# The gate-up combination of the sampled rows, issued one feature pair later

## The chip, the core and the metric

The kernel runs on one core of one Trainium2 chip. The metric is the device time of one execution in microseconds; the times given for a kernel are of several executions, and the median is the one to compare.

## The reference, cut to what matters

A two-layer decoder trunk is applied to 512 prompt rows and to 32 sampled rows (8 sequences of 4), both of width 1024. Each layer has a mixing part (four token mixers, an input and an output projection) and a feed-forward part. The change touches the feed-forward part of the sampled rows alone:

```python
gate, up = jnp.split(rms_norm(x, p['g_ffn_pre']) @ p['w_gu'], 2, axis=-1)
x = x + rms_norm((jax.nn.silu(gate) * up) @ p['w_down'], p['g_ffn_post'])
```

`w_gu` is 1024 x 5632 (2816 gate columns, then 2816 up columns), `w_down` is 2816 x 1024. In the kernel a feature is a block of 128 of the 2816 columns, so there are 22, handled two at a time as a feature pair.

## The kernel before

**The prompt rows** set the shape of the feed-forward stage. `prompt` walks over the features in three chunks (0 to 7, 8 to 15, 16 to 21). For each pair f, f+1 it loads 1 MB of gate weights and 1 MB of up weights into the two buffers of `raw` (SyncE issues the loads, line 202), splits each into a high and a low part (`whi` by ScalarE on line 194, `wlo` by VectorE on line 197), and multiplies: `dense_fm` makes 24 products of 512 columns per feature and side, 96 for a pair. All matmuls are issued by the helper on line 128; in the rows these products write `acc`. ScalarE and VectorE then form silu(gate) times up (`th`, lines 1368 to 1370) and split it (`h`, lines 1372 and 1373). After each chunk the down projection follows (`project`, or `project_last` for the third chunk), with its own weights through `raw` (line 214).

**The sampled rows** go beside this. For features 0 to 9 a background generator (`sample_ffn`) loads its own weights (`rws`). From feature F0 = 10 on, the sampled rows use the weights which the prompt rows have in `raw` already: `raw_cols` calls `gate_up(f, 0)` on the gate weights and `gate_up(f, 1)` on the up weights before it splits them. Each call makes 8 small float32 products with `quads`, every one into 32 rows of a PSUM tile with tag `sx` (three banks); the trace shows each float32 product as two records, so a call has 16. ScalarE copies the 128 x 256 sum into a half of `obm` (line 1208), a tile of tag `g_s`, which has two buffers.

**The combination** of a pair is `swiglu`. Four float32 products (8 records) with 32 columns of constants add up the four row groups and turn the result, with `obm` as the weights that are loaded; they write `o2`, a PSUM tile of tag `ps` (two banks). ScalarE takes the tanh (`sth`, line 1178), and two VectorE instructions form silu(gate) times up (lines 1179 and 1180) into the 64 columns of `hsa` or `hsb` that `hs2(f)` names. The down projection of the sampled rows reads these columns: `down(c0)` and `also(half)` run `quads` on each raw tile of `w_down`, with `hsa` or `hsb`, and the raw tile can be loaded again only after them and the split.

**The order on an engine** is not the order of the text. The context on line 1484 is opened with `schedule_with_timeline_sim=True`: the instructions of the whole program are put in order before it runs. What the order came to is read from the trace. Once fixed, each engine keeps to it.

In layer 0 the pairs 10, 12 and 14 close the second chunk and the pairs 16, 18 and 20 make up the third; layer 1 is the same. This gives 6 combinations a layer that the change touches, 12 in all.

Of the kernel before, what the change touches and what calls it, by code (L numbers as in the profile page):

```python
# [50 lines left out]
F0 = 10  # L51
# [71 lines left out]
def trunk(ctx, tc, A, O):  # L123
# [3 lines left out]
    def mm(out, lhsT, rhs, start=True, stop=True):  # L127
        T.matmul(out, lhsT, rhs, start=start, stop=stop)  # L128
# [13 lines left out]
    def ps():  # L142
        return psx("ps")

    def psx(tag):
        pool, bufs = banks[tag]
        return pool.tile([128, 512], F32, tag=tag, bufs=bufs, name=tag)
# [17 lines left out]
    def x_at(stage):  # L165
        if stage == 0:
            return x_in
        if stage == 2 * DEPTH:
            return y_out
        return lambda r0, n: xm[stage - 1][r0:r0 + n, :]  # L170
# [73 lines left out]
    def finish_sample(fp, parts, m_s, x_t, stage, gpo, gpr, dst, tag):  # L244


        ss = fp.tile([128, 4], F32, name="sums_s")[:NT]
        junk = fp.tile([128, DM], BF16, name="junk_s")
        for half in range(2):
            o = ps()  # L250
            mm(o[:NT, :], selkg, parts[half])
            hs = slice(512 * half, 512 * half + 512)
            S.activation(junk[:NT, hs], o[:NT, :], AF.Square, accum_out=ss[:, half:half + 1])
            V.tensor_tensor(m_s[:, hs], o[:NT, :], gpo[:NT, hs], op=ALU.mult)
        V.tensor_tensor(ss[:, 2:3], ss[:, 0:1], ss[:, 1:2], op=ALU.add)
        r = rsqrt(fp, ss[:, 2:3], NT, 1, 1.0 / DM, RMS_EPS, tag)
        V.scalar_tensor_tensor(x_t, m_s, r, x_t, op0=ALU.mult, op1=ALU.add)
        SY.dma_start(x_at(stage + 1)(SEQ, NT), x_t)
        if gpr is None:
            return  # L260
        S.activation(junk[:NT], x_t, AF.Square, accum_out=ss[:, 3:4])
        r = rsqrt(fp, ss[:, 3:4], NT, 1, 1.0 / DM, RMS_EPS, tag)
        V.scalar_tensor_tensor(m_s, x_t, r, gpr[:NT], op0=ALU.mult, op1=ALU.mult)
        if dst is None:
            turn(m_s, NT, SEQ)
            return
        for b in range(2):
            o = ps()
            ov = o[:, :4 * NT].rearrange("p (c t) -> p c t", c=4)
            for c in range(4):  # L270
                T.transpose(ov[:, c, :], m_s[:, 128 * (4 * b + c):128 * (4 * b + c) + 128], ident[:NT, :NT])
            S.copy(dst[:, 4 * b:4 * b + 4, :], ov)
# [886 lines left out]
    def sample_ffn(l, cmn, sp, ys, hs_in, share):  # L1159


        def pso():
            return psx("sx")

        def narrow(w, act, groups, c0, n, out):

            for gi, (k0, nk) in enumerate(groups):
                rw = sp.tile([128, 4, 256], F32, tag="rw", bufs=RWB, name="rws")
                SY.dma_start(rw[:, :nk, :n], w[128 * k0:128 * (k0 + nk), c0:c0 + n].rearrange("(k p) f -> p k f", p=128))
                quads(out, act, rw, k0, 0, nk, gi == 0, n, [q for _, q in groups[gi + 1:]])  # L1170
                yield

        def swiglu(ob, dst):
            o2 = ps()
            for i in range(4):
                mm(o2[:, NT * i:NT * i + NT], ob[:, 128 * i:128 * i + 128], selkg)
            t = sp.tile([128, 2 * NT], F32, tag="sth", bufs=2, name="sth")
            S.activation(t, o2[:, 0:2 * NT], AF.Tanh, scale=0.5)  # L1178
            V.scalar_tensor_tensor(t, t, 1.0, o2[:, 0:2 * NT], op0=ALU.add, op1=ALU.mult)  # L1179
            V.scalar_tensor_tensor(dst, t, 0.5, o2[:, 2 * NT:4 * NT], op0=ALU.mult, op1=ALU.mult)  # L1180

        g8 = [(0, 4), (4, 4)]
        gpo = sp.tile([128, DM], F32, tag="g_s", bufs=2, name="g_s")[:NT]
        SY.dma_start(gpo, A["g_mix_post"][l, :].partition_broadcast(NT))
        gpr = sp.tile([128, DM], F32, tag="g_s", bufs=2, name="g_s")[:NT]
        SY.dma_start(gpr, A["g_ffn_pre"][l, :].partition_broadcast(NT))
        m_s = sp.tile([128, DM], F32, tag="m_s", name="m_s")[:NT]
        x_t = sp.tile([NT, DM], F32, name="x_s")
        SY.dma_start(x_t, x_at(2 * l)(SEQ, NT))
        finish_sample(sp, share["parts"], m_s, x_t, 2 * l, gpo, gpr, hs_in, "s")  # L1190
        yield

        m4 = sp.tile([128, DM], F32, tag="m_s", name="m4")
        G.memset(m4, 0.0)
        hsa = sp.tile([128, 16, NT], F32, name="hsa")
        hsb = cmn.tile([128, 8, NT], F32, tag="ys", name="hsb")
        hs = lambda k: hsa[:, k, :] if k < 16 else hsb[:, k - 16, :]
        hs2 = lambda k: (hsa[:, k:k + 2, :] if k < 16 else hsb[:, k - 16:k - 14, :]).rearrange("p f t -> p (f t)")
        obs = {}

        def gate_up(f, i):
            def run(r):
                if i == 0:
                    obs[f] = sp.tile([128, DM], F32, tag="g_s", bufs=2, name="obm")
                o = pso()
                for gi in range(2):
                    quads(o, lambda k: hs_in[:, k, :], r[:, 4 * gi:4 * gi + 4, :], 4 * gi, 0, 4, gi == 0, 256, (4,) if gi == 0 else ())
                S.copy(obs[f][:, 256 * i:256 * i + 256], o[:, :256])
                if i == 1:
                    swiglu(obs.pop(f), hs2(f))  # L1210
            return run

        def down(c0):
            def run(r, k0, nk):
                i0 = max(0, F0 - k0)
                if i0 < nk:
                    o = pso()
                    quads(o, hs, r, k0, i0, nk, True, 512)
                    P = slice(32 * i0, 32 * nk)
                    V.tensor_tensor(m4[P, c0:c0 + 512], m4[P, c0:c0 + 512], o[P, :], op=ALU.add)  # L1220
            return run

        share.update(gate_up=gate_up, down=down, hs=hs)
        wgu = A["w_gu"][l]
        for fp in range(F0 // 2):
            ob = cmn.tile([128, 512], F32, tag="pr", bufs=2, name="ob")
            for i in range(2):
                o = pso()
                yield from narrow(wgu, lambda k: hs_in[:, k, :], g8, DFF * i + 256 * fp, 256, o)
                S.copy(ob[:, 256 * i:256 * i + 256], o[:, :256])  # L1230
            swiglu(ob, hs2(2 * fp))
            yield
        groups = [(k, min(4, F0 - k)) for k in range(0, F0, 4)]
        for cb in range(4):
            o = pso()
            yield from narrow(A["w_down"][l], hs, groups, 256 * cb, 256, o)
            c = slice(256 * cb, 256 * cb + 256)
            P = slice(0, 32 * min(4, F0))
            V.tensor_tensor(m4[P, c], m4[P, c], o[P, :256], op=ALU.add)
            yield  # L1240
        while "last" not in share:
            yield
        share["m4"] = [cmn.tile([128, 512], F32, tag="pr", bufs=2, name="m4h") for _ in range(2)]
        for i in range(2):
            S.copy(share["m4"][i], m4[:, 512 * i:512 * i + 512])
        yield

    def quads(out, act, w, k0, i0, nk, first, n, later=()):


        for i in range(i0, nk):
            mm(out[32 * i:32 * i + 32, :n], act(k0 + i), w[:, i, :n], start=first, stop=all(q <= i for q in later))
# [77 lines left out]
    def prompt(l, fp, share):  # L1330
# [19 lines left out]
        for ci, (f0, nf) in enumerate(chunks):  # L1350
            hb = [yp.tile([128, 2, 2, SEQ], F32R, tag="y", name="h") for _ in range(nf // 2)]
            for fpair in range(nf // 2):
                f = f0 + 2 * fpair
# [10 lines left out]
                for i, c0, n, tag in parts:  # L1364
# [8 lines left out]
                    V.tensor_tensor(hb[fpair][:, 1, i, c0:c0 + n], th[:, :n], hh.bitcast(F32), op=ALU.subtract)  # L1373
                    yield 0.02 * n
            act = lambda k, h, ts_: hb[k // 2][:, h, k % 2, ts_]
            if ci < len(chunks) - 1:
                yield from project(A["w_down"][l], f0, nf, act, m, ci == 0, share)
                continue
# [50 lines left out]
    for l in range(DEPTH):  # L1429
# [5 lines left out]
        with tc.tile_pool(name=f"ffn{l}", bufs=1, reuse_waits="tile") as fp, \  # L1435
# [3 lines left out]
            share = {}  # L1439
# [46 lines left out]
```

## Time and profile before

| | us |
|---|---|
| median of 3 runs | 1473.05 |
| lowest and highest of them | 1468.88 and 1478.08 |
| the profiled execution | 1468.52 |
| its span, first to last instruction | 1466.7 |
| TensorE busy in it | 1399.7 |
| VectorE, ScalarE, GpSimd busy | 819.1, 498.2, 252.2 |

All durations in the text come from the one profiled execution. Its span leaves out what lies before the first and behind the last instruction, 1.8 us. Starts are counted from the begin of the span. TensorE's weight loads (PEld) are listed apart from its matmuls (PE) and overlap them. The end of a matmul is modelled, so that two neighbours overlap in the list: what a matmul costs is read from start to start.

### The profile page before, as it was taken

What the parts mean: (1) busy time and instruction counts of PE and PEld (TensorE: products, weight loads), DVE (VectorE), ACT (ScalarE), POOL (GpSimd) and SP (SyncE); (2) the same over time, 40 slices, a digit from 0 to 9 for tenths busy, and PEclk for the clock granted to TensorE, in tenths of its full rate; (3) what the DMA queues carried; (4) which work ended last, traced back from release to release, by engine and by line L of the source; (5) the groups of instructions that cost most, each with busy time, mean ns of one, the idle gap of its engine ahead of it and who ended that gap; (6) DMA issues with size and microseconds to landing.
All of it is one profiled execution on the core that took longest, in us unless ns stands there. A gap on an engine that the chain in (4) does not pass through costs nothing.

```text
span 1466.7 us, 22999 instructions
## 1 busy us (share of the span) xinstructions
PE 1399.7 (95%) x9274; PEld 1091.6 (74%) x9274; DVE 819.1 (56%) x1624; ACT 498.2 (34%) x978; POOL 252.2 (17%) x271
## 2 busy tenths in 40 slices
PE   6999898999999999999989997989999999999997
PEld 6987687766676777777789876877666677777775
DVE  4996677866424323433769856778664333333344
ACT  4346453322224221222433444543222332222231
POOL 1001155354200000000310011543542000000003
PEclk9999898999999999999999978999999999999999
DMA  6320335787759741323432203367877596213132
GB/s 206 101 88 30 125 129 181 266 292 274 263 179 298 230 137 58 106 67 130 151 123 73 73 29 123 126 218 250 307 277 272 182 300 212 99 58 115 58 133 90
DMA packets 155204, 235.60 MB, mean 161 GB/s; under 512 B 8880, under 2 KB 116410, under 8 KB 155098
## 3 DMA queue, kind: packets, MB, share of 16 engines
q1 hardware_dynamic: 136522, 166.76, 34.6%
q0 software_dynamic: 18432, 67.12, 12.6%
q8 instruction: 73, 1.20, 0.3%
q14 instruction: 33, 0.27, 0.1%
q10 hardware_dynamic: 144, 0.26, 0.0%
HBM read 222.07 MB, written 12.04 MB: 160 GB/s over the span
## 4 chain that ended last, share of the span: by engine, by line
PE 80%; DVE 9%; issue 4%; DMA 2%; ACT 2%; POOL 2%; another core or an unknown queue 1%; SPq 0%; POOLq 0%; DVEq 0%; ACTq 0%
PE acc L128 61%; PE sx L128 10%; PE ps L128 3%; PE s L128 3%; DVE sca L897 2%; DVE wlo L197 1%; PE oT L128 1%; DMA kr<-in_cache_k_dram,ik 1%; POOL rsw L178 1%; DVE m L1326 1%; ACT whi L194 1%; DVE x_t L1319 1%; PE ps L521 1%; PE ps L239 1%
## 5 line engine op out<-in xcount | busy, mean ns | idle before, releaser
L128 PE MATMUL acc<-xhi,whi 128*128 128x512 f32 (+2 forms) x1152 | 410.8, 358 | 3.1 <-issue 1.1
L128 PE MATMUL acc<-xhi,wlo 128*128 128x512 f32 (+2 forms) x1152 | 407.9, 354 | 1.0 <-issue 0.7
L128 PE MATMUL acc<-xlo,whi 128*128 128x512 f32 (+2 forms) x1152 | 407.4, 354 | 1.3 <-DVE xlo L242 1.1
L197 DVE TENSOR_TENSOR wlo<-raw,whi 128x1024 fp32r<-128x1024 f32 x172 | 216.5, 1265 | 187.4 <-ACT whi L194 185.9
L194 ACT CAST whi<-raw 128x1024 fp32r<-128x1024 f32 x178 | 184.8, 1048 | 381.6 <-PE acc L128 324.0
L128 PEld LDWEIGHTS acc<-xhi,whi 128*128 128x128 f32 x1152 | 221.1, 192 | 47.5 <-issue 13.3
L128 PEld LDWEIGHTS acc<-xhi,wlo 128*128 128x128 f32 x1152 | 221.1, 192 | 34.9 <-issue 8.7
L128 PEld LDWEIGHTS acc<-xlo,whi 128*128 128x128 f32 x1152 | 221.3, 192 | 32.8 <-issue 5.3
L128 PE MATMUL acc<-whi,h 128*128 128x512 f32 x704 | 225.4, 397 | 0.3 <-issue 0.3
L128 PEld LDWEIGHTS acc<-whi,h 128*128 128x128 f32 x704 | 132.0, 189 | 45.4 <-issue 11.8
L128 PE MATMUL acc<-wlo,h 128*128 128x512 f32 x352 | 139.2, 397 | 0.0
L1301 POOL TENSOR_TENSOR m<-m,g_g_ffn_post 128x512 f32<-128x512 f32 x14 | 20.0, 1435 | 509.1 <-ACT junk L1300 509.1
L1014 DVE STREAM_TRANSPOSE kt<-kr 128x1024 f32<-128x1024 f32 x64 | 78.3, 1232 | 40.5 <-remote 18.2
L427 DVE SCALAR_TENSOR_TENSOR cacc<-hext,pf,cacc 128x512 f32<-128x512 f32 x120 | 86.9, 746 | 0.8
L1011 POOL DMA_INDIRECT kr<-in_cache_k_dram,ik x64 | 68.6, 1072 | 101.8 <-DVE kt L1014 88.1
L128 PEld LDWEIGHTS acc<-wlo,h 128*128 128x128 f32 x352 | 66.5, 189 | 17.6 <-issue 4.1
L178 POOL TENSOR_TENSOR rsw<-rsw,mhalf 128x1 f32<-128x1 f32 (+2 forms) x62 | 37.3, 604 | 239.4 <-DVE rsw L177 223.4
L1041 POOL DMA_INDIRECT vr<-in_cache_v_dram,iv x64 | 62.1, 970 | 82.0 <-PE sx L128 66.5
L1370 DVE SCALAR_TENSOR_TENSOR th<-th,acc 128x512 f32<-128x512 f32 (+1 forms) x46 | 29.7, 645 | 80.7 <-PE acc L128 80.5
L128 PE MATMUL sx<-kt,qs 128*32 128x128 f32 x1024 | 49.9, 277 | 7.7 <-issue 6.1
L128 PEld LDWEIGHTS sx<-kt,qs 128*32 128x32 f32 x1024 | 30.7, 109 | 24.5 <-issue 18.8
L1179 DVE SCALAR_TENSOR_TENSOR sth<-sth,ps 128x64 f32<-128x64 f32 x22 | 4.8, 219 | 72.7 <-ACT sth L1178 72.7
(426 smaller groups left out, 1855.2 us busy)
## 6 DMA issues: line engine op xcount, KB each, us to landing
raw<-in_w_gu_dram SPq DMA_DIRECT2D x44, 1024.0 KB
raw<-in_w_down_dram SPq DMA_DIRECT2D x20, 1024.0 KB
rws<-in_w_gu_dram SPq DMA_DIRECT2D x40, 512.0 KB
raw<-in_w_in_dram SPq DMA_DIRECT2D x16, 1024.0 KB
raw<-in_w_out_dram SPq DMA_DIRECT2D x8, 1024.0 KB
rwo<-in_w_out_dram SPq DMA_DIRECT2D x16, 512.0 KB
rws<-in_w_down_dram SPq DMA_DIRECT2D x16, 512.0 KB
x<-x_t SPq DMA_DIRECT2D x12, 512.0 KB
```

The source lines that it names most:

```text
L128: T.matmul(out, lhsT, rhs, start=start, stop=stop)
L178: G.tensor_tensor(y, v, mhalf[:P, :n], op=ALU.pow)
L194: S.copy(hi, src)
L197: eng.tensor_tensor(lo, src, hi.bitcast(F32), op=ALU.subtract)
L239: T.transpose(ov[:, c, :], src[:P, 128 * (4 * b + c):128 * (4 * b + c) + 128], ident[:P, :P])
L427: V.scalar_tensor_tensor(a, hext[c][:, t:t + SEQ], pf[:, 8 + 2 * t + c:9 + 2 * t + c], a, op0=ALU.mult, op1=ALU.add)
L897: V.scalar_tensor_tensor(a[:, c], ext[:, c, :, t:t + 4], pf[:, 8 + 2 * t + c:9 + 2 * t + c], a[:, c], op0=ALU.mult, op1=ALU.add)
L1011: G.indirect_dma_start(out=kr, out_offset=None, in_=ck, in_offset=bass.IndirectOffsetOnAxis(ap=ik[:, s, bg:bg + 1], axis=0))
L1014: V.transpose(kt, kr)
L1041: G.indirect_dma_start(out=v.rearrange("p t e -> p (t e)"), out_offset=None, in_=cv, in_offset=bass.IndirectOffsetOnAxis(ap=iv[:, s, a:a + ...
L1301: (V if (t, half) == (3, 1) else G).tensor_tensor(m[t][:, hs], m[t][:, hs], gain[:, hs], op=ALU.mult)
L1370: V.scalar_tensor_tensor(th[:, :n], th[:, :n], 0.5, ou[:, :n], op0=ALU.mult, op1=ALU.mult)
```

## The change

`gate_up` no longer runs `swiglu` when the up half of `obm` is copied. It puts the pair in a list, `late`. The list is emptied by `flush`, which runs `swiglu` on what it finds: at the next call of `gate_up`, behind its products and ahead of its copy, or, for the last pair of a chunk, ahead of the down projection.

```diff
@@ gate_up
                 for gi in range(2):
                     quads(o, lambda k: hs_in[:, k, :], r[:, 4 * gi:4 * gi + 4, :], 4 * gi, 0, 4, gi == 0, 256, (4,) if gi == 0 else ())
+                flush()
                 S.copy(obs[f][:, 256 * i:256 * i + 256], o[:, :256])
                 if i == 1:
-                    swiglu(obs.pop(f), hs2(f))
+                    late.append((obs.pop(f), f))
             return run
+
+        late = []
+
+        def flush():
+
+            while late:
+                ob, f = late.pop()
+                swiglu(ob, hs2(f))
+
+        share["flush"] = flush
@@ prompt, behind the loop over the pairs of a chunk
             act = lambda k, h, ts_: hb[k // 2][:, h, k % 2, ts_]
+            if f >= F0:
+                share["flush"]()
             if ci < len(chunks) - 1:
                 yield from project(A["w_down"][l], f0, nf, act, m, ci == 0, share)
```

## Rows read from the trace of the kernel before

**Rows 1.** The page: TensorE's busy time and its granted clock in 40 slices.
```profile
PE 1399.7 (95%) x9274; PEld 1091.6 (74%) x9274; DVE 819.1 (56%) x1624; ACT 498.2 (34%) x978; POOL 252.2 (17%) x271
...
PEclk9999898999999999999999978999999999999999
```

**Rows 2.** Busy time in two stretches: PE, PEld, DVE, ACT, POOL, clock, DMA share, GB/s.
```profile
600.00:690.00 90.00, 90.00 (x473) 71.18 (x472) 32.30 (x41) 23.86 (x35) 0.00 (x0) 1.00 0.27 91
...
1320.00:1380.00 60.00, 60.00 (x318) 46.89 (x313) 22.44 (x29) 14.87 (x22) 0.00 (x0) 1.00 0.32 105
```

**Rows 3.** Waits of TensorE's matmuls, 440 to 760 us: total, times, longest.
```profile
PE ps L239 <- DVE rsw L177: 3.9, 1, 3.9
PE acc L128 <- ACT hext L374: 1.0, 1, 1.0
```

**Rows 4.** The tile obm, whole run: who waited for it, us and times.
```profile
ACT sth L1178: 44.6, 10
PEld acc L128: 2.5, 6
```

**Rows 5.** Timeline of TensorE, pair 16 of layer 0: start, us, instruction.
```profile
615.72 1.93 PE L128 MATMUL sx<-raw,hs_in 128*32 128x256 f32 x32
617.59 0.50 PE L128 MATMUL acc<-xhi,whi 128*128 128x512 f32 x1
...
620.70 0.40 PE L128 MATMUL acc<-xlo,whi 128*128 128x512 f32 x1
620.93 0.53 PE L128 MATMUL ps<-cst,obm 128*128 128x32 f32 x4
621.30 0.47 PE L128 MATMUL acc<-xhi,wlo 128*128 128x512 f32 x1
621.61 0.40 PE L128 MATMUL acc<-xhi,whi 128*128 128x512 f32 x1
...
622.08 0.53 PE L128 MATMUL ps<-cst,obm 128*128 128x32 f32 x4
...
640.93 1.93 PE L128 MATMUL sx<-raw,hs_in 128*32 128x256 f32 x32
```

**Rows 6.** Timeline of TensorE: combinations of the background's pairs beside quads, layer 0.
```profile
482.81 0.63 PE L128 MATMUL ps<-cst,ob 128*128 128x32 f32 x4
483.37 1.93 PE L128 MATMUL sx<-raw,hs_in 128*32 128x256 f32 x32
...
510.80 0.39 PE L128 MATMUL acc<-xhi,wlo 128*128 128x512 f32 x1
511.03 0.97 PE L128 MATMUL ps<-cst,ob 128*128 128x32 f32 x8
511.93 1.07 PE L128 MATMUL sx<-rws,hsa 128*32 128x256 f32 x16
```

**Rows 7.** Timeline of ScalarE, pair 16 of layer 0; in brackets the idle time before.
```profile
617.72 0.37 ACT L1208 COPY obm<-sx 128x256 f32<-128x256 f32 x1 [0.49 <-PE sx L128]
622.64 0.22 ACT L1178 ACTIVATE sth<-ps 128x64 f32<-128x64 f32 x1 [4.54 <-PE ps L128]
```

**Rows 8.** Timeline of VectorE, pair 16 of layer 0.
```profile
623.15 0.22 DVE L1180 SCALAR_TENSOR_TENSOR hsb<-sth,ps 128x64 f32<-128x64 f32 x1
```

**Rows 9.** Timeline of TensorE where the third chunk's products end, layer 0.
```profile
691.07 0.40 PE L128 MATMUL acc<-xhi,wlo 128*128 128x512 f32 x1
691.39 1.91 PE L128 MATMUL sx<-raw,hsb 128*32 128x512 f32 x12
...
703.60 0.51 PE L128 MATMUL acc<-whi,h 128*128 128x512 f32 x1
```

**Rows 10.** The chain that ended last, 690 to 712 us: start, us, what.
```profile
692.52 5.12 DMA raw<-in_w_down_dram
...
697.66 1.05 ACT whi L194
...
699.88 1.23 DVE wlo L197
```

## The prediction

> **What bounds the kernel now.** I read the page first. TensorE is busy for 1399.7 of 1466.7 us at full granted clock in all but a few slices, and no other engine comes near [rows 1]. Busy is an average, so the table of stretches came next, for the stretches in which the 12 moved combinations lie. In both stretches shown, one for each layer, TensorE is busy for the whole of it (90.00 of 90 us and 60.00 of 60 us), at clock 1.00, with VectorE and ScalarE at about a third and a quarter [rows 2]. The ends of matmuls are modelled, so a busy engine could still hide waits; two further views settle this. The list of waits has two matmul waits between 440 and 760 us, 3.9 and 1.0 us, and neither is in the feature pairs: one follows line 177, the other line 374, both in the passage to the next layer [rows 3]; the same view from 1230 us to the end, layer 1, has none. And the timeline of a pair accounts for itself: pair 16 takes 640.93 - 615.72 = 25.21 us. Its 32 quad records take 617.59 - 615.72 = 1.87 us. Its 96 products start 620.93 - 620.70 = 0.23 us apart, which makes 22.1 us. That leaves 1.2 us; two combination halves (0.9 us, below) and the passages to and from the quads (0.1 us each) account for 1.1 of it [rows 5], and the rest is less than the rounding of the pitch. Nothing is left for a wait. In this stage the time is the sum of TensorE's own instructions, and a change there counts only as it changes that sum or makes TensorE wait.
>
> The reader is also to see where the combination stands **now**. By the text it comes ahead of the pair's 96 products, and with the engine in text order it would wait for the copy of `obm`. In the trace it doesn't stand there. The copy of the up half starts at 617.72 [rows 7], the products go on from 617.59, and the two halves of the combination come among them at 620.93 and 622.08 [rows 5]. So the order made before the run has pulled the products ahead of it and the copy is covered already. The long waits charged to `obm` are ScalarE's: 44.6 us in 10 waits of its tanh [rows 4], such as the 4.54 us of pair 16 [rows 7]. They are idle time of an engine with a quarter of the work. TensorE's weight loads waited 2.5 us, 6 times [rows 4], but a weight load that overlaps a running product costs nothing, and the matmul list has no such wait.
>
> **The change part by part.**
>
> It *removes* the place of the combination among its own pair's products. One half costs what stretches the products around it: 621.30 - 620.93 = 0.37 us to the next product, and that product takes 621.61 - 621.30 = 0.31 instead of 0.23, so 0.45 us in all [rows 5]; two halves are 0.9 us, 12 times in the run. The wait that this placing might have saved is 0, from the two paragraphs above. A gain from there is at most the 2.5 us of weight loads, if none of it were covered; I take 0, since the matmul rows show no gap.
>
> It *adds* the same 8 records elsewhere. By the new text they come behind the next pair's gate quads and ahead of its up quads. In the trace an instruction that is ready goes in the order of the text (gate and up quads together as soon as the previous products end, at 615.72 and again at 640.93, then the products [rows 5]). The weights `obm` of the pair before will have lain ready for some 20 us. So I expect gate quads, 8 records, up quads, in 8 of the 12 places (pairs 10, 12, 16 and 18 of two layers). The trace has one half of a background combination in that very neighbourhood, between quads: 483.37 - 482.81 = 0.56 us for 4 records [rows 6]. Eight records in a row take 511.93 - 511.03 = 0.90 us behind products [rows 6]. From below, then, a combination between quads costs 0.56 + (0.90 - 0.37) = 1.1 us, and from above twice 0.56 plus a dear entry and exit, about 0.1 us (products to quads take 691.39 - 691.07 = 0.32 instead of 0.23, rows 9), so 1.3 us. Against 0.9 us that is +0.2 to +0.4 us, 8 times: **+1.6 to +3.2 us**. I take 1.2 us each and +2.4 us, as the row at 482.81 is the nearest.
>
> [...]
>
> In the 4 other places (pairs 14 and 20 of two layers), `flush` comes behind the chunk's products and ahead of the down projection. The eight records at 511.03 are that case: products before, quads after. They cost 0.90 us, and spare the 0.1 us of passage from products to quads, so 0.8 to 0.9: **0 to -0.1 us each**; I take 0.
>
> **Behind the move at the end of a chunk.** The down quads read what the combination makes. For pair 16 the chain from the second half to the result is 623.15 + 0.22 - 622.08 = 1.29 us [rows 5, 8]. Today the result of pair 20 is ready long before the quads at 691.39 [rows 9]. After the change, the 8 records go first, which makes all of these quads 0.9 us later. Those of features 20 and 21, the last 4 of the 12 records, would then start near 693.5 (691.39 + 0.9 + 8 x 0.15); the second half would start near 691.8 and give its result 1.29 us later, at 693.1, in time. But the raw tiles are loaded again behind these quads: the load at 692.52 takes 5.12 us, then come the two splits [rows 10]. They would be some 0.9 us later. The first low part is there at 699.88 (the next split starts as it ends), and the products of the second half of the columns start around 703.60 at the earliest that the order of records lets me see [rows 9, 10]. The room is about 3.7 us, so 0.9 us is covered: **0**, and if that cover were gone, up to 0.9 us a layer. At the end of the second chunk the reload is for a half that is used after some 20 us of products; nothing there.
>
> **Queues passed.** The copy of the next gate half now stands in the text behind the tanh of the pair before; on ScalarE it may wait some 1.5 us for it. Behind it in the queue are splits, which have to wait for products today as well. Who waits for the copy is the next combination, 25 us on, and one of three `sx` banks. Two buffers hold `obm`; both are now in use at once, and the third pair needs the first buffer one pair after it came free. VectorE gets its two 0.22 us instructions [rows 8] later. No DMA and nothing on GpSimd moves. I cost all this at 0; the cover is an idle ScalarE (three quarters of the stretch, rows 2).
>
> **Sum:** +2.4 us with bounds of -0.4 and +5.0 (3.2 us, with 0.9 us uncovered in each layer). Against the profiled execution, 1468.52 + 2.4 = 1470.9. That execution was 4.5 us below the median of the runs shown, and its span leaves out 1.8 us that the change doesn't touch. On the median, 1473.05 + 2.4 = **1475.5 us**, +0.16%. A measurement of this kernel can hardly tell less than 1% from no change, and its three runs alone lie 9.2 us apart.
>
> **The rivals.**
>
> *The combination costs the same wherever it stands.* The records are the same, and the 0.90 us for eight in a row [rows 6] equals the two halves of 0.45 us [rows 5]. [...] Against it stands the 0.56 us between quads. It gives 1473, within 1 us. The same time results if the order made before the run doesn't move the combination as the text does, that is, if the change doesn't do what it says.
>
> *The late combination holds up the down weights (slower).* The place is the start of the third chunk's down projection, twice in the run. If the order puts the down quads not 0.9 us later but behind the first turn of products (18 of them at 0.23 us, 4.2 us), the reload and its splits come 5 us later, against 3.7 us of room. It decides from 3.7 us on; the price is 1.4 us a layer there, and at most the whole of the 5.12 us load [rows 10]. With the 2.4 us of the forecast this is +5 to +13 us, 1478 to 1486. For it: this chain passes through the load today. Against it: ready quads come ahead of products in the text, and the quads of features 16 to 19 don't need the late result.
>
> *A luckier order (faster).* The edit makes the order anew, downstream too. The idle time that it could close is the 4.9 us at the passage to layer 1 [rows 3] and its like; 1468 if all of it went. Nothing in the change aims there.
>
> **How the numbers follow.** Forecast 0.55, equal cost 0.25, slower by the down weights 0.10, luckier order 0.06, and 0.04 for an order that costs over 1% in places that I can't name. Only part of the last two goes beyond 1%, on either side: faster 0.03, within 1% 0.92, slower 0.05. The forecast's own span is 1472.6 to 1478. The runs scatter by 4 to 5 us about their median, half of which I allow a median; with the rivals this makes 1467 to 1483.
>
> **What would show it.** In the timeline of TensorE the 8 `obm` records would stand together between 16 and 16 quad records, with 1.1 to 1.3 us from their first start to the next quad; the period of pair 18 would be 25.4 to 25.6 us; ScalarE's wait for the tanh would be gone from its list without any gain in the span. TensorE would stay 100% busy in the same stretches. Wrong would be a pair shorter than 25.0 us, a wait of matmuls around 700 us, or a shift in the mixing stages larger than all this.

## The result, and the profile after

The changed kernel takes 1481.64 us (median of 12 runs, 1475.4 to 1483.85), the kernel before 1469.95 us (12 runs, 1465.55 to 1478.08). The ratio of the two, taken where both ran side by side, is 1.0066, with an interval of 1.0050 to 1.0082 (that of the two medians is 1.0080): 7 to 12 us slower, 9.7 us in the middle. That is within 1%, as forecast, but four times the 2.4 us that the forecast had for the change. The profiled execution took 1483.85 us, its span 1482.1.

The page gives TensorE's totals and its granted clock in 40 slices [rows 1].

```profile
PE 1404.8 (95%) x9274; PEld 1091.6 (74%) x9274; DVE 818.6 (55%) x1624; ACT 498.6 (34%) x978; POOL 250.7 (17%) x271
...
PEclk9999898999999999999999998999999999999999
```

The work is the same (9274 matmuls). The table of stretches, with the columns of [rows 2], shows the feature pairs and the stretches in which the third chunk ends.

```profile
600.00:690.00 90.00, 90.00 (x467) 70.57 (x466) 28.84 (x37) 22.37 (x33) 0.00 (x0) 1.00 0.27 88
690.00:720.00 30.00, 27.16 (x118) 17.14 (x117) 14.30 (x19) 8.85 (x13) 1.27 (x1) 0.94 0.50 170
...
1320.00:1380.00 60.00, 60.00 (x303) 46.37 (x301) 22.59 (x26) 15.99 (x20) 0.00 (x0) 1.00 0.22 71
1420.00:1450.00 30.00, 26.79 (x122) 17.75 (x122) 13.33 (x18) 7.45 (x12) 1.27 (x1) 1.00 0.15 54
```

TensorE is as full as before among the pairs, but idle for about 3 us right behind the third chunk, in both layers. The list of its waits names them: from 440 to 760 us the first three lines, against [rows 3], and from 1230 us to the end the last one beside the same 1.5 and 1.3 us.

```profile
PE ps L239 <- DVE m L1337: 5.5, 1, 5.5
PE acc L128 <- ACT whi L194: 1.5, 1, 1.5
PE sx L128 <- issue: 1.3, 1, 1.3
...
PE ps L128 <- DVE m4h L1406: 0.3, 1, 0.3
```

The long wait at `obm`, 44.6 us before [rows 4], is gone. This is who waits for the tile now:

```profile
ACT sth L1178: 5.2, 10
```

Nothing was gained by it. The timeline of TensorE shows the combination where it was forecast (pair 18, against [rows 5]) and then what happens where the third chunk's products end (against [rows 9]).

```profile
643.69 1.07 PE L128 MATMUL sx<-raw,hs_in 128*32 128x256 f32 x16
644.69 1.08 PE L128 MATMUL ps<-cst,obm 128*128 128x32 f32 x8
645.70 1.07 PE L128 MATMUL sx<-raw,hs_in 128*32 128x256 f32 x16
...
669.18 1.07 PE L128 MATMUL sx<-raw,hs_in 128*32 128x256 f32 x16
...
694.35 0.39 PE L128 MATMUL acc<-xhi,wlo 128*128 128x512 f32 x1
694.58 0.97 PE L128 MATMUL ps<-cst,obm 128*128 128x32 f32 x8
695.48 1.07 PE L128 MATMUL sx<-raw,hsb 128*32 128x512 f32 x8
697.80 1.90 PE L128 MATMUL sx<-raw,hsb 128*32 128x512 f32 x4 [1.26 <-issue]
...
708.53 0.73 PE L128 MATMUL acc<-whi,h 128*128 128x512 f32 x2 [1.53 <-ACT whi L194]
```

The period of pair 18 is 669.18 - 643.69 = 25.49 us, against 25.21 for pair 16 before [rows 5] and 25.23 for pair 18 (640.93 to 666.16): 0.26 to 0.28 more. At the chunk's end the eight records come first, then 8 of the 12 down quads; the last four wait 1.26 us, and the second half of the columns waits 1.53 us for its splits. ScalarE, VectorE and SyncE show why:

```profile
678.09 1.05 ACT L194 CAST whi<-raw 128x1024 fp32r<-128x1024 f32 x1 [5.38 <-PE acc L128]
...
695.50 0.62 ACT L1383 CAST h<-th 128x512 fp32r<-128x512 f32 x1 [5.64 <-DVE th L1381]
696.02 0.22 ACT L1178 ACTIVATE sth<-ps 128x64 f32<-128x64 f32 x1
696.14 1.98 ACT L194 CAST whi<-raw 128x1024 fp32r<-128x1024 f32 x2
...
706.82 0.63 ACT L1311 ACTIVATE junk<-m 128x512 bf16<-128x512 f32 x1 [4.20 <-DVE m L1309]
707.45 2.93 ACT L194 CAST whi<-raw 128x1024 fp32r<-128x1024 f32 x3
```

```profile
696.14 0.69 DVE L1384 TENSOR_TENSOR h<-th,h 128x512 fp32r<-128x512 f32 x1 [0.68 <-ACT h L1383]
696.75 0.22 DVE L1179 SCALAR_TENSOR_TENSOR sth<-sth,ps 128x64 f32<-128x64 f32 x1
696.88 0.68 DVE L1406 TENSOR_TENSOR m4h<-m4h,sx 128x512 f32<-128x512 f32 x1
697.48 0.22 DVE L1180 SCALAR_TENSOR_TENSOR hsb<-sth,ps 128x64 f32<-128x64 f32 x1
...
700.35 2.35 DVE L197 TENSOR_TENSOR wlo<-raw,whi 128x1024 fp32r<-128x1024 f32 x2
```

```profile
695.63 0.34 SPq L183 DMA_DIRECT2D g_g_mix_pre<-in_g_mix_pre_dram  x1
...
699.73 0.38 SPq L214 DMA_DIRECT2D raw<-in_w_down_dram  x1
...
702.72 0.38 SPq L214 DMA_DIRECT2D raw<-in_w_down_dram  x1
```

In the kernel before, ScalarE's timeline has all three casts of the first half of the down weights together, right behind the early tanh:

```profile
673.20 2.94 ACT L194 CAST whi<-raw 128x1024 fp32r<-128x1024 f32 x3
...
697.66 2.94 ACT L194 CAST whi<-raw 128x1024 fp32r<-128x1024 f32 x3 [4.82 <-DMA raw<-in_w_down_dram]
700.51 0.63 ACT L1300 ACTIVATE junk<-m 128x512 bf16<-128x512 f32 x1
```

The first half's casts (673.20) are 17.9 us ahead of the last dense product (691.07, rows 9). Now two of the three stand right behind the *late* tanh, at 696.14, that is 1.8 us behind that product (694.35). What follows is late too: the low parts, the reload of `raw` (699.73, which is 5.4 us behind the last dense product, against 692.52 - 691.07 = 1.5 [rows 9, 10]) and the second half's casts (707.45, 13.1 us behind it, against 697.66 - 691.07 = 6.6). The chain that ended last shows how they hang together:

```profile
697.80 1.92 PE sx L128 x4
...
706.03 0.70 DVE m L1309
...
706.82 0.72 ACT junk L1311 x2
707.54 0.94 ACT whi L194
```

The first reload goes out as the last four quads end (697.80 + 1.92 = 699.72), so it is the eight records and the late result that delay it, and not the casts; the second (702.72) goes out as the low parts end (700.35 + 2.35). The second half's casts wait for neither reload by the trace: they stand in ScalarE's order behind `junk` (706.82), which waits for the sum `m` that VectorE makes when the first half's products end. In the kernel before, the same casts stood ahead of `junk` (697.66 and 700.51) and waited for the load.

In layer 1, where the clock stayed at 1.00, the eight records (0.9 us) and TensorE's three waits (1.3, 0.3 and 1.5 us) are 4.0 of the 4.8 us that the stretch behind the third chunk lost; the next table has this stretch as tail 1.

A table by stage, from start to start in TensorE's timeline, locates the loss. *Pairs* runs from the first quad of pair 10 to the last dense product of pair 20. *Tail 0* runs from that product in layer 0 to the first mixing product of layer 1, *tail 1* from that product in layer 1 to the end of the span. The kernels of the experiments are added; ratios are to the kernel before in the same session, that is, timed beside it.

```
                            pairs 0  tail 0  pairs 1  tail 1  ratio  interval
before                       207.70   47.36   207.70   48.21
before, profiled again       207.70   47.04   207.70   48.20
changed                      208.74   54.76   208.74   52.96  1.0066 1.0050-1.0082
changed, again               208.74   53.55   208.74   52.99  1.0103 1.0055-1.0152
pair 20 at once              209.59   47.89   209.59   47.90  1.0060 1.0042-1.0078
only pair 20 late            206.81   53.57   206.81   52.92  1.0058 1.0036-1.0080
pairs 14 and 20 at once      208.51   48.03   208.51   48.21  0.9998 0.9982-1.0013
late, both tiles elsewhere   208.74   49.15   208.74   49.44  1.0000 0.9986-1.0014
late, obm elsewhere          208.74   53.91   208.75   52.90  1.0128 1.0063-1.0193
late, sth elsewhere          208.74   51.24   208.74   50.87  one run
late, pad in layer 1         208.74   53.43   208.74   52.91  one run
before + hold obm            207.70   50.58   207.70   50.01  1.0034 1.0019-1.0049
before + hold obm and sth    207.70   50.81   207.70   50.00  1.0047 1.0029-1.0065
ahead of the gate quads      208.34   53.44   208.34   50.80  one run
```

The pairs repeat to a hundredth of a microsecond in both layers. The change costs them 1.04 us a layer, and the tails 6.2 to 7.4 and 4.8 us (0.9 of it in each is pair 20's combination, which moved there): 13.0 us by the second profile of the changed kernel and the first of the kernel before.

### The profile page after: what moved, and what is told of

It is laid out like the page before. It is cut to its first block, busy times and chain, and to the rows that moved or that the text cites. A ratio compares the mean times of both kernels' runs of the same rounds, so it can differ in the third digit from the quotient of the medians.

```text
span 1482.1 us, 22996 instructions
## 1 busy us (share of the span) xinstructions
PE 1404.8 (95%) x9274; PEld 1091.6 (74%) x9274; DVE 818.6 (55%) x1624; ACT 498.6 (34%) x978; POOL 250.7 (17%) x271
## 4 chain that ended last, share of the span: by engine, by line
PE 78%; DVE 9%; issue 4%; DMA 3%; ACT 3%; POOL 1%; another core or an unknown queue 1%; SPq 0%; DVEq 0%; POOLq 0%; ACTq 0%
PE acc L128 60%; PE sx L128 9%; PE ps L128 3%; PE s L128 3%; DMA kr<-in_cache_k_dram,ik 2%; DVE sca L897 2%; DVE wlo L197 1%; PE oT L128 1%; DVE kt L1014 1%; ACT whi L194 1%; PE ps L521 1%; DVE m L1337 1%; DVE x_t L1330 1%; PE ps L239 1%
## 5 line engine op out<-in xcount | busy, mean ns | idle before, releaser
L1383 ACT CAST h<-th 128x512 fp32r<-128x512 f32 (+1 forms) x48 | 27.9, 582 | 58.9 <-DVE th L1381 54.2
```

The costliest lines, as they stand in the source:

```text
L1383: S.copy(hh, th[:, :n])
```

## The experiments

**Which pair is it?** The theory: the loss is pair 20's, whose late combination keeps memory of the background's pool (`sff`) in use while the down projection's pool (`trb`), with the split weights, wants to take it over. The rival: the lag as such.

The edit of the first kernel; the second has `f != 20`.

```diff
                     late.append((obs.pop(f), f))
+                    if f == 20:
+                        flush()
```

> The changed kernel, but pair 20 is combined at once, as before; the other five pairs of a layer stay late. Tail below is the time from the start of the last product of pair 20 in layer 1 to the end of the span: 48.2 us before, 53.0 us after the change. Theory (the late combination of pair 20 is the loss, at the start of the third chunk's down projection): tail 48 to 49 us, whole kernel 1 to 4 us above the kernel before (ratio 1.001 to 1.003). Rival (the loss is the dearer place between the quads, or the end of the second chunk): whole kernel 7 us or more above the kernel before, tail whatever.

> The kernel before with pair 20 alone combined late, behind the third chunk's products; the other five pairs of a layer are combined at once. Theory (pair 20 is the loss): tail of layer 1 52 to 54 us instead of 48.2, whole kernel 7 to 12 us above the kernel before. Rival (place between the quads, end of the second chunk): at most 2 us above, tail 48 to 49.

Measured: with pair 20 at once the tails are 47.9 and 47.9 us again, with pair 20 alone late 53.6 and 52.9. The loss in the tails is pair 20's alone. The first kernel is nevertheless 0.6% slower than before, where the theory had 1 to 4 us and the rival 7 or more: of its 8.7 us the stages explain about 4, 3.8 of them in the pairs. The rest has to lie in the mixing, whose order was made anew as well. In its profiled execution the mixing of layer 1 took 468.7 us, against 455.6 in the second profile of the kernel before, and the granted clock fell to 0.65 in part of it (840 to 860 us). How much is order and how much is clock, no run settles. Nor do the two kernels' losses add up: 8.7 and 8.4 us are more than the change's 9.7.

**Is it the memory, or the late result?** One kernel keeps pair 20 late but puts its `obm` and `sth` into other pools. The other is the kernel before with one unread product on `obm`, behind the third chunk.

```diff
-            t = sp.tile([128, 2 * NT], F32, tag="sth", bufs=2, name="sth")
+            t = cmn.tile([128, 2 * NT], F32, name="sthl") if own else sp.tile([128, 2 * NT], F32, tag="sth", bufs=2, name="sth")
-                    obs[f] = sp.tile([128, DM], F32, tag="g_s", bufs=2, name="obm")
+                    obs[f] = yp.tile([128, DM], F32, tag="y", name="obl") if f == 20 else sp.tile([128, DM], F32, tag="g_s", bufs=2, name="obm")
```

> The changed kernel, pair 20 late as in it, but its two sums and its tanh lie in tiles of pools that stay open, so that the tiles of the last stage (ring of split weights, rows of gains, residual rows), which take over the memory of the sampled rows' pool, don't wait for them. Theory A (the held memory is the loss: splits of the third chunk's down weights, and through them the reload, wait for it): the two splits come back ahead of the last products, tail of layer 1 48.5 to 50 us, whole kernel 2 to 5 us above the kernel before. Theory B (the late result is the loss: the last down quads wait for it, and the reload for them): tail 52 to 54 us, whole kernel 8 to 12 us above.

```diff
+            if f == 20:
+                o = psx("ps")
+                mm(o[:, :NT], share["held"][:, :128], selkg)
```

> The kernel before, all combinations at once, with one more small product behind the third chunk's products in each layer, which reads the sums of pair 20 and whose result nobody reads: it holds their memory as long as the change does, and delays no result. Theory A (held memory): tail of layer 1 51 to 53 us instead of 48.2, splits of two of the three down weights of the first half start only behind the last products, whole kernel 5 to 10 us above the kernel before. Theory B (late result): tail 48 to 49 us, whole kernel at most 1 us above.

With both tiles elsewhere the tails are 49.15 and 49.44 us, and the time is that of the kernel before, where theory A had 2 to 5 us more. Pairs and tails together still have 5 us more; where they were given back isn't shown (the mixing of layer 1 took 455.9 us in this profile and 455.6 in the second one of the kernel before). ScalarE's timeline has the two casts back ahead of the late tanh (TensorE goes from the first 8 quads, 681.15, straight to products, 682.15):

```profile
661.13 2.00 ACT L194 CAST whi<-raw 128x1024 fp32r<-128x1024 f32 x2 [2.75 <-DMA raw<-in_w_down_dram]
...
681.70 0.22 ACT L1178 ACTIVATE sthl<-ps 128x64 f32<-128x64 f32 x1
```

So where the tiles lie is the larger part of the loss, and the late result the smaller: 1.2 to 1.8 us, of which 0.9 is the combination itself. The result is as late as in the changed kernel, but with the casts early TensorE has products to do until it comes. The hold alone costs 3.2 and 1.8 us in the tails (50.0 us in layer 1, where theory A had 51 to 53) and 4.9 us in the whole, just under its 5 to 10.

**Held memory, or the order?** In the kernel with the hold on `obm`, the two casts came late, but in layer 0 still ahead of the product that holds the tile. A hold on both tiles repeats this:

```diff
-                mm(o[:, :NT], share["held"][:, :128], selkg)
+                mm(o[:, :NT], share["held"][:, :128], share["heldt"][:, :NT])
```

> The kernel before, and one unread product (2 records) behind the third chunk's products that reads both tiles of pair 20's combination, the gathered sums (obm) and the tanh (sth). The earlier kernel held obm alone, and two of the three first-half splits of the down weights still came ahead of the last dense product; in the changed kernel they stood behind it, right after the tanh. Theory (the memory of both tiles passes to the split weights and the gains): those two splits come behind the unread product, near the last dense product plus 1 to 2 us, and the tails are 51.5 to 54 us in both layers, close to the changed kernel's 53.0 and 54.8 less the late result's share of 1.2 to 1.8. Rival (the tanh's tile plays no part): as with obm alone, 50.0 to 50.6 us.

ScalarE in layer 0 and in layer 1, then, of layer 0, TensorE's holding product and SyncE's load of the next gain:

```profile
674.89 1.99 ACT L194 CAST whi<-raw 128x1024 fp32r<-128x1024 f32 x2
...
1397.74 2.00 ACT L194 CAST whi<-raw 128x1024 fp32r<-128x1024 f32 x2 [5.10 <-PE ps L128]
```

```profile
679.72 0.30 PE L128 MATMUL ps<-sth,obm 128*128 128x32 f32 x2
```

```profile
680.10 0.34 SPq L183 DMA_DIRECT2D g_g_mix_pre<-in_g_mix_pre_dram  x1
```

The tails are 50.8 and 50.0 us, as with `obm` alone. In layer 1 the casts do wait for the product, 5.10 us. In layer 0 they run 4.8 us ahead of it, so that no held memory can have kept them there: they only stand later in ScalarE's order. What does wait there is the load of the gain `g_mix_pre`, which goes out right behind the product. This agrees with the layout of the pools: `obm` of pair 20 lies in layer 1 under the first split weights and in layer 0 only under that gain. By the same layout `sth` lies under nothing of the new pool; no trace shows that. Three kernels then moved one tile at a time, or pushed the split weights of layer 1 off `obm`:

```diff
+                if l + 1 == DEPTH:
+                    pad = tp.tile([128, DM], F32, name="pad")
+                    V.memset(pad[:1, :1], 0.0)
```

> The changed kernel, with only the gathered sums of pair 20 (obm) in memory of their own; the tanh tile (sth) stays in the background's pool, whose memory the tiles of the down projection take over. Theory A (a tile of the closed pool that is still in use holds back the order: the instructions on the new pool's tiles are put behind the last use of any tile of the closed pool, whether or not they share addresses): the two first-half splits stay behind the late tanh on ScalarE and the tails stay at 53 to 55 us in both layers. Theory B (only the memory itself holds: the splits wait where they lie on obm's addresses): with obm moved away the tails fall to about 49.2 to 49.5 us, as with both tiles moved.

> The changed kernel, with an unused tile of 4 KB a partition put into layer 1's down-projection pool, so that there, too, no split weight lies on obm's addresses (in layer 0 that is so already; the load of the next gain lies on them). Theory A (order, not addresses): layer 1's tail stays at 52.5 to 54 us with the two splits still behind the late tanh. Theory B (the addresses): layer 1's tail falls to about 49.4 us. Layer 0, which is unchanged, stays at 53 to 55 us by both.

> The complement: the changed kernel with only the tanh tile of pair 20 in memory of its own, obm in the background's pool. Theory A (either tile is enough to hold back the order): tails of 53 to 55 us, as in the changed kernel. Theory B': if it is the tanh tile alone that counts, about 49.2 to 49.5 us.

With `obm` elsewhere the tails stay at 53.9 and 52.9 us, with the pad at 53.4 and 52.9, and the casts stay behind the late tanh. So theory B, by which the addresses of `obm` are what holds the casts, falls; that none are shared with `sth` is shown for layer 0 alone, where the casts ran ahead of a product that reads both tiles. With `sth` elsewhere they are 51.2 and 50.9, between the two expectations. There, too, the casts stand right behind the late tanh on ScalarE (starts 693.87 and 693.75), but TensorE takes a product ahead of the last four quads, so that they no longer stand idle for the late result:

```profile
694.95 0.50 PE L128 MATMUL acc<-whi,h 128*128 128x512 f32 x1 [0.68 <-ACT whi L194]
695.53 1.05 PE L128 MATMUL sx<-raw,hsb 128*32 128x512 f32 x4
```

Either tile in the closed pool is enough to put the casts behind the late tanh; the rest of the price depends on how the order falls out behind them. Apart from the two holds, all kernels here agree with this. In the six in which pair 20's late combination uses a tile of that pool, the casts stand right behind the late tanh in both layers. In the other four, in which it uses none or isn't late, they stand ahead of the last dense product.

**The price of the place.** One kernel lags only between quads (pairs 10, 12, 16, 18); one puts the combination ahead of the gate quads.

```diff
+                    if f in (14, 20):
+                        flush()
```

> Pairs 10, 12, 16 and 18 are combined one pair late, pairs 14 and 20 at once, as in the kernel before. Theory (the place between quads costs 0.28 us a pair, the loss at the end of the third chunk comes from pair 20 alone): the stage of pairs 10 to 20 takes 207.7 + 4 x 0.28 = 208.8 us in each layer, the tails stay at 47.4 to 48.2 us, ScalarE's first-half splits of the down weights stand ahead of the last dense product, and the whole is about 2 us (0.15%) above before, plus what a remade order adds in the mixing of layer 1 (seen as a stage of its own). Rival (the lag itself, not pair 20, upsets the end of the third chunk): tails above 50 us.

```diff
+                flush()
                 o = pso()
                 for gi in range(2):
                     ...
-                flush()
                 S.copy(obs[f][:, 256 * i:256 * i + 256], o[:, :256])
```

> As the changed kernel, but the combination of the pair before stands ahead of the gate quads instead of between gate and up quads. If the place between two groups of quads is what makes it dearer (one exit from quads and one entry more), the period of a pair falls from 25.49 to 25.1 to 25.2 us, since the combination then has dense products before it and quads behind it, and spares the passage from the one to the other. If eight records cost more wherever they stand one behind the other, the period stays at 25.4 to 25.5 us. [...]

The first has 208.51 us for the pairs, 0.81 more than before (0.20 a pair and not the 0.28 that was expected), and normal tails. Its time is that of the kernel before (0.9998, with an interval that ends 1.9 us above it), where about 2 us more were expected. The second's timeline:

```profile
603.71 1.93 PE L128 MATMUL sx<-raw,hs_in 128*32 128x256 f32 x32
...
627.96 0.97 PE L128 MATMUL ps<-cst,obm 128*128 128x32 f32 x8
628.86 1.93 PE L128 MATMUL sx<-raw,hs_in 128*32 128x256 f32 x32
```

Its period is 25.15 us against 25.49 between quads: eight records cost 0.90 us behind products and 1.01 between quads. That the rest is paid by the split run of quads, which is entered and left once more, is argued and not tested by itself.

**Do the same kernels repeat?** Both were profiled again.

> The kernel before, profiled beside the next kernels. Mixing of layer 1 (from the first mixing product of layer 1 to the first gate product of its pair 10) was 472.4 us in the first profile of before and 455.9 to 468.7 us in the kernels profiled since. If the place of the run (another chip) accounts for the lower figures, this profile has about 456 to 458 us there; if the order made before the run accounts for them, it has 472 again. The stage of pairs 10 to 20 should be 207.70 us in both layers and the tail behind its last dense product 47.4 to 48.2 us.

> The changed kernel again, profiled and timed beside these. Pairs 10 to 20 take 208.74 us in each layer. If the low clock behind the third chunk of layer 0 (0.94 from 690 to 720 us) belongs to that one execution, the tail of layer 0 is now near layer 1's 53 us; if it belongs to the waits there, it is 54.8 us again. The whole is 0.4 to 0.9% above before.

The kernel before had a span of 1438.5 us in this other session, with the same 207.70 us for the pairs and 455.6 instead of 472.4 us for the mixing of layer 1: that stage can't be compared between sessions. The changed kernel has 53.55 instead of 54.76 us in tail 0; the low clock there belongs to the first execution (in the second the clock was 1.00 from 685 to 715 us). Its ratio, 1.0103, is above the 0.4 to 0.9% that was expected, but its interval reaches down to 0.55%.

## Why the prediction was right or wrong

**The range: held, in part by luck.** 1481.64 us lies within 1467 to 1483, which allowed for scatter and rivals, but outside the forecast's own span of 1472.6 to 1478. Some of that span's width has no term behind it: the low ends of the terms add up to +1.2 us (1.6 - 0.4) and not to -0.4. The base moved as well, from 1473.05 us (3 runs) to 1469.95 (12 runs). One sign of being wrong that the prediction had named did appear: matmuls wait around 700 us, 1.26 us at 697.80 and 1.53 us at 708.53.

**Where TensorE stands: right.** The pairs are bound by its own instructions; ScalarE's 39 us less of waiting for `obm` gained nothing.

**Where the combination goes, and its price: right, at the low end.** Gate quads, eight records, up quads, as forecast, in three of the four places a layer; behind pair 12's records come two products and then the up quads (543.09, 544.00 and 544.64). Pair 18 costs 0.26 to 0.28 us more, against the +0.3 that was taken. The parts differ: 1.01 us to the next quad instead of 1.1 to 1.3, and the rest, as argued above, on the passages beside it. Over the pairs 10, 12, 16 and 18 this is 0.81 us a layer, 1.6 us for all eight places, the lower bound. The rival of equal cost falls with it, by the stage alone: the pairs repeat to 0.01 us, while the whole time can't tell 1.6 us. The Trainium skill ("TensorE: Matmul & The Clock Gate", section "LDWEIGHTS (loading the stationary operand)") gives a weight load its number of columns over 1.2, in nanoseconds; by that, eight loads of 128 columns take an estimated 0.85 us. The runs here have 0.90 us for the eight records behind products and 1.01 between quads, so the measured times are used: in this kernel the place counts.

**Pair 14's end of a chunk, taken at 0: wrong, +1.1 us a layer** (209.59 with it late, 208.51 with it at once). Products were expected ahead of it; the timeline of the changed kernel has quads of the down projection there (12 records, then the eight, then 8 quads).

**Pair 20's end of a chunk, taken at 0: wrong, and most of the loss.** The step that failed reads "They would be some 0.9 us later", of the reload and the splits behind it. The reload came 3.9 us later (5.4 against 1.5 us behind the last dense product) and the casts behind it 6.5 us later (13.1 against 6.6); without the low clock, in the second profile, 3.1 and 5.4 us (reload at 693.77, casts at 701.30, last dense product at 689.24). The room of 3.7 us was overrun: of the 6.5 us, 1.53 us came out as TensorE's wait for these casts; it had lost time ahead of them already. The path was another than the one through the reload: the new order has these casts behind `junk` and so behind the end of the first half's products. What the prediction missed besides is a step ahead of the reload: the casts of the *first* half, which it left where they were, 18 us ahead. It took from the text of the change that the combination's result is late, and didn't ask what else is ordered by the life of its tiles. The pool that holds them is closed and its memory handed on, and the order made before the run kept two of the new pool's first casts behind the last use of the old pool's tiles. That the casts return when both tiles are elsewhere is shown, and that the addresses of `obm` aren't the reason; by which rule the order is made is not.

**The late result: wrong by a queue.** It was expected 1.29 us behind the second half, in time for the last four quads. ScalarE had the cast of `h` ahead of the tanh, and VectorE two instructions of 0.69 and 0.68 us in the way. The result was ready at 697.70, 3.1 us after the first of the eight records, and the quads waited 1.26 us. The wait shows because the casts were late as well: with both tiles elsewhere TensorE filled the time with products.

**The rival "the late combination holds up the down weights"** named the place, the point from which it decides and a time (1478 to 1486) that held 1481.64, with a chance of 0.10. Its route, quads put behind products, isn't the one that was taken.

**The sum by stages**, 2 x 1.04 + 6.2 + 4.8 = 13.0 us, lies a little above the interval of the first comparison (7 to 12 us) and within that of the second (8 to 22). What the mixing gave back in the first, if anything, isn't shown.

## What to carry over

Before an instruction is put later, list every tile that it reads or writes and ask which pool they belong to, which pool takes over its memory, and what of that one stands behind their last use in each engine's order: the price here was paid by casts 18 us away that read none of these tiles. At the end of a stage, a result's delay has to be walked through the queues of the other engines, entry by entry. A wait that disappears from an engine with a third of the work is no gain.

## What the runs showed of the hardware

**The granted clock is not a property of the program alone.** The kernel before in its two profiles; the second is 12 us ahead there, so the same work starts at 820 us in the first and at 808 us in the second:

```profile
820.00:860.00 40.00, 40.00 (x277) 34.87 (x275) 24.09 (x63) 21.14 (x50) 2.85 (x3) 0.85 0.20 68
```

```profile
808.00:848.00 40.00, 40.00 (x310) 34.44 (x309) 28.30 (x74) 23.66 (x58) 2.84 (x3) 1.00 0.20 68
```

The same instructions ran at full clock (2.4 GHz) in one and at 0.50 (1.2 GHz) from about 849 to 865 us in the other, where TensorE had been busy at 1.00 in each 2 us from 832 to 848. It cost 7.5 us: VectorE's instructions are 12.0 us later than their counterparts at 831 us and 19.5 us later at 871 us (times of the first profile). Likewise in the changed kernel four quads took 1.90 us behind a wait of 1.26 us (clock 0.50 from 698 to 700 us), and in its second profile, behind the same wait, 1.05 (clock 1.00):

```profile
692.69 1.05 PE L128 MATMUL sx<-raw,hsb 128*32 128x512 f32 x4 [1.25 <-issue]
```

Much of the scatter from run to run comes with it: in a line fitted to the timed runs whose clock is listed, about the mean of their kernel and session, 0.001 less of mean granted clock goes with 0.85 us more of span, and the scatter falls from 2.9 to 1.8 us. By that line the kernel with pairs 14 and 20 at once (mean clock 0.985 against 0.982 before) would be 2.1 us slower at equal clock, where its stages have 1.6 in the pairs and up to 1 in a tail. This is a correlation, not an experiment.
